# Matmul with rotary embedding on one core: load order, PSUM banks as single tiles, halves and stores at the end

## The chip, the core and the metric

The kernel runs on one core of a Trainium2 chip. The core has five engines that run their own instruction queues side by side and meet at semaphores: TensorE (PE in the profile; matmuls and transposes), VectorE (DVE), ScalarE (ACT), GpSimd (POOL) and SyncE (SP, which here only issues transfers). SBUF is the working memory, PSUM the eight accumulation banks that TensorE writes; a bank holds 512 float32 numbers in each of 128 partitions. Transfers between HBM and SBUF are issued from the queues of SP, ACT and POOL.

The metric is the device time of one execution in microseconds. Six executions of the kernel before took 158.26 to 159.04, with a median of 158.5.

## What is computed

```python
# x: (16, 512, 768)   weight: (768, 768)   cos, sin: (512, 64)   n_heads = 12, all float32
y = np.matmul(x, weight).reshape(batch, seq, n_heads, head_dim)      # head_dim = 64
y1, y2 = y[..., :32], y[..., 32:]
out1 = y1 * cos1 - y2 * sin1      # cos1, sin1: the first 32 columns of cos and sin
out2 = y2 * cos2 + y1 * sin2      # cos2, sin2: the last 32
out = np.concatenate([out1, out2], axis=-1).reshape(batch, seq, hidden)
```

## The kernel before

**Tiles.** The 8192 rows of x are cut into 64 tiles of 128 rows, and the tiles are taken in 32 pairs (n, s), n from 0 to 31 and s 0 or 1. The two tiles of a pair belong to two batches and the same positions, so they share cos and sin. The contraction over 768 is cut into six chunks of 128, named (t, e). Below, x00 is the tile (0, 0), w0 the first chunk of the weight.

**One tile's way.** load() fetches a tile as float32 on SP's queue (L81). cast() makes it float16 (xc), on ACT for all but two early tiles. transpose() turns it with six TensorE transposes into a PSUM tile pt (L124) and copies that to SBUF as xT (L74 on ACT, L76 on VectorE). Every third pair from 8 on (BLOCKS: 8, 11, ... 29) goes another way: POOL's queue loads it as float16 in 32-row blocks (L103), and VectorE transposes it (L131); it costs TensorE nothing. mm() (L167) multiplies one chunk of a tile with one chunk of the weight, w_sb, which cast_w() (L111) has made float16 on VectorE. rope() (L181, VectorE) multiplies the sums in PSUM by cos and by the signed, swapped sin, which gives tq with twice as many columns; add() (L192, POOL) adds the two halves of tq into ov; store() (L241) sends ov to HBM.

**PSUM.** psum() gives a pair one tile of three banks, psy; there are two of these, and pt_pool holds two more banks. The first tile of a pair fills bank 0 and half of bank 1, the second the rest. All three banks come free together, when rope_pair() has read the last of them. The last four pairs (ALONE = 4) take two banks for each tile, 512 columns and 256, from psy or, for three of the eight tiles, from pt_pool (psz in the profile).

**Start.** SP issues the first four x tiles, then w0 in two pieces of 256 and 512 columns, then w1 to w5, cos, sin, and the x tiles of pairs 2 to 6. TensorE begins with matmuls on zeros (warm(), L251, 17 in all), with the transposes of the first four tiles between them. It takes each weight chunk as it arrives: both tiles of pair 0 in every step, tile (1, 0) for four chunks beside them. What is left of pair 1 comes after w5, then pair 2.

**Order.** The order on each engine is the order of the code. In the main loop over pairs 2 to 31 each tile's twelve matmuls are followed by upto("turn", ...) and upto("cast", ...), which emit the transposes and casts of later tiles. Both run ahead by two and four tiles, and from index 31 on by up to six tiles more: the line `k += min(6, max(0, k - 31) // 4)`. The pool of xT tiles has 11 buffers for this. After a pair's matmuls rope_pair() emits the multiplication and the add of the pair; the store of pair n-3 goes out on ACT's queue just before. Pairs 26 and 27 are multiplied and added in halves of 768 columns.

**End.** In the last four pairs each tile is multiplied by rope_alone(), in pieces of 512 and 256 columns, added as 768 columns and stored from ACT. Stores 25 to 27 stand before these on ACT. The last tile (31, 1) is done by rope_last(): the 256 columns by VectorE and POOL with a store on ACT, the 512 by three VectorE instructions (L220 twice, L224) with a store on SP.

Of the kernel before, what the change touches and what calls it, by code (L numbers as in the profile page):

```python
# [10 lines left out]
FP32 = mybir.dt.float32  # L11
FP16 = mybir.dt.float16
# [5 lines left out]
def kernel(  # L18
# [9 lines left out]
    nc = tc.nc  # L28
# [6 lines left out]
    R = 32  # L35
    NQ = P // R
    NT = H // (2 * P)
    SB = S // P
    NP = B * SB // 2
    CHUNKS = [(t, e) for t in range(NT) for e in range(2)]  # L40
# [20 lines left out]
    xpool = ctx.enter_context(tc.tile_pool(name="xpool", bufs=10))  # L61
    bpool = ctx.enter_context(tc.tile_pool(name="bpool", bufs=5))
    cpool = ctx.enter_context(tc.tile_pool(name="cpool", bufs=6))
    tpool = ctx.enter_context(tc.tile_pool(name="tpool", bufs=11))
    rpool = ctx.enter_context(tc.tile_pool(name="rpool", bufs=3))
    opool = ctx.enter_context(tc.tile_pool(name="opool", bufs=6))
    pt_pool = ctx.enter_context(tc.tile_pool(name="pt", bufs=2, space=bass.MemoryType.PSUM))
    py_pool = ctx.enter_context(tc.tile_pool(name="py", bufs=2, space=bass.MemoryType.PSUM))

    xss, xhs, x16, xTT, psys, tqs, ovs = {}, {}, {}, {}, {}, {}, {}  # L70

# [47 lines left out]

    def transpose(n, s, eng):  # L120
        xc = x16.pop((n, s)).rearrange("p (t m e) -> p t e m", t=NT, e=2)
        pt = pt_pool.tile([P, NT, 2, P], FP16, tag="pt", name="pt")
        for t, e in CHUNKS:
            nc.tensor.transpose(pt[:, t, e, :], xc[:, t, e, :], ident)  # L124
        xT = tpool.tile([P, NT, 2, P], FP16, tag="xT", name="xT")
        copy(eng, xT, pt)
        xTT[n, s] = xT
# [12 lines left out]


    def psum(n, s):
        if n < NP - ALONE:
            if n not in psys:
                psys[n] = py_pool.tile([P, 3, 512], FP32, tag="psy", name="psy")
            cut = 512 if s == 0 else 256
            return [
                (psys[n][:, s, ds(s * 256, cut)], 0, cut),
                (psys[n][:, s + 1, 0 : H - cut], cut, H),
            ]  # L150
        if (n, s) not in psys:
            if (2 * (n - NP + ALONE) + s) % 3 == 1:
                psys[n, s] = [
                    pt_pool.tile([P, 512], FP32, tag="pt", name="psz") for _ in (0, 1)
                ]
            else:
                ps = py_pool.tile([P, 3, 512], FP32, tag="psy", name="psy")
                psys[n, s] = [ps[:, 0], ps[:, 1]]
        lo, hi = psys[n, s]
        return [(lo, 0, 512), (hi[:, 0 : H - 512], 512, H)]  # L160

    def mm(n, s, t, e, c0=0, c1=H):
        for k, (ps, lo, hi) in enumerate(psum(n, s)):
# [11 lines left out]
    def rope(n, c0, c1, ps):  # L175
        r = n % SB
        nh = (c1 - c0) // D
        if n not in tqs:
            tqs[n] = rpool.tile([P, 2, 2 * H], FP32, tag="tq", name="tq")
            ovs[n] = opool.tile([P, 2 * H], FP32, tag="ov", name="ov")  # L180
        nc.vector.tensor_tensor(  # L181
            out=tqs[n][:, :, c0:c1].rearrange("p j (h d) -> p j h d", d=D),
            in0=ps.rearrange("p (h d) -> p h d", d=D)
            .unsqueeze(1).broadcast_to((P, 2, nh, D)),
            in1=csn[:, :, r, :].unsqueeze(2).broadcast_to((P, 2, nh, D)),
            op=MULT,
        )

    def add(n, c0, c1, eng):
        w = c1 - c0  # L190
        tq = tqs[n][:, :, ds(c0, w)]
        eng.tensor_tensor(  # L192
            out=ovs[n][:, ds(c0, w)].rearrange("p (h t d) -> p h t d", t=2, d=HD),
            in0=tq[:, 0].rearrange("p (h t d) -> p h t d", t=2, d=HD),
            in1=tq[:, 1].rearrange("p (h t d) -> p h t d", t=2, d=HD)[:, :, ::-1, :],
            op=ADD,
        )

    def rope_pair(n, step=2 * H):
        ps = psys[n].rearrange("p b n -> p (b n)")  # L200
        for c in range(0, 2 * H, step):
            rope(n, c, c + step, ps[:, ds(c, step)])
            add(n, c, c + step, nc.gpsimd)

    def rope_alone(n, s):
        for ps, lo, hi in psum(n, s):
            rope(n, s * H + lo, s * H + hi, ps)

    def rope_last(n, s):
        (ps, _, cut), (pz, _, _) = psum(n, s)
        c0, c1, c2 = s * H, s * H + cut, (s + 1) * H
        rope(n, c1, c2, pz)
        add(n, c1, c2, nc.gpsimd)
        nh = cut // D
        q = tqs[n][:, 1, c0:c1]
        ph = ps.rearrange("p (h d) -> p h d", d=D)
        for o, j in ((q.rearrange("p (h d) -> p h d", d=D), 1), (ph, 0)):
            nc.vector.tensor_tensor(  # L220
                out=o, in0=ph, op=MULT,
                in1=csn[:, j, n % SB, :].unsqueeze(1).broadcast_to((P, nh, D)),
            )
        nc.vector.tensor_tensor(  # L224
            out=ovs[n][:, c0:c1].rearrange("p (h t d) -> p h t d", t=2, d=HD),
            in0=ps.rearrange("p (h t d) -> p h t d", t=2, d=HD),
            in1=q.rearrange("p (h t d) -> p h t d", t=2, d=HD)[:, :, ::-1, :],
            op=ADD,
        )
        store(n, nc.sync, c0, c1)  # L230
        store(n, nc.scalar, c1, c2)

    def store(n, eng, c0=0, c1=2 * H):
        b, r = where(n, 0)
        dst = out.rearrange("b (p r) h -> r p b h", r=SB)[r, :, b : b + 2]
        src = ovs[n].rearrange("p (b h) -> p b h", b=2)
        if c1 - c0 < 2 * H:
            s = c0 // H
            dst = dst[:, s, c0 - s * H : c1 - s * H]
            src = src[:, s, c0 - s * H : c1 - s * H]  # L240
        eng.dma_start(out=dst, in_=src)  # L241
# [5 lines left out]
    def warm(k):  # L247
        for _ in range(k):
            n, b = divmod(opened[0] % 6, 3)
            psum(n, 0)  # L250
            nc.tensor.matmul(  # L251
                psys[n][:, b], cold[:, 0:P], cold, start=True, stop=opened[0] < WARM - 6
            )
            opened[0] += 1

    ctx.enter_context(tc.manual_schedule())

# [8 lines left out]
        pattern=[[-1, P]],  # L266
        channel_multiplier=1,
    )
    for n in (0, 1):
        load_pair(n)  # L270
    load_w(0, 0, 0, 256)
    load_w(0, 0, 256, H)
    for t, e in CHUNKS[1:]:
        load_w(t, e)
    nc.sync.dma_start(out=csn[:, 0], in_=cos.rearrange("(p r) d -> p r d", r=SB))
    nc.sync.dma_start(out=sin_sb, in_=sin.rearrange("(p r) d -> p r d", r=SB))
    for n in range(2, AHEAD):
        load_pair(n)

    done = {"cast": 4, "turn": 4}

    def upto(what, k):
        k += min(6, max(0, k - 31) // 4)
        while done[what] < min(k, 2 * NP):
            n, s = divmod(done[what], 2)
            done[what] += 1
            if what == "cast":
                if n not in BLOCKS:  # L290
                    cast(n, s, nc.scalar)
            elif n in BLOCKS:
                transpose_blocks(n, s)
            else:
                transpose(n, s, nc.scalar)

    warm(10)
    cast(0, 0, nc.vector)
    cast(0, 1, nc.scalar)
    transpose(0, 0, nc.vector)  # L300
    warm(2)
    transpose(0, 1, nc.scalar)
    cast(1, 0, nc.vector)
    cast(1, 1, nc.scalar)
    warm(2)
    transpose(1, 0, nc.vector)
    warm(3)
    for c0, c1 in ((0, 256), (256, H)):
        cast_w(0, 0, c0, c1)
        mm(0, 0, 0, 0, c0, c1)  # L310
        mm(0, 1, 0, 0, c0, c1)
        if c0 == 0:
            transpose(1, 1, nc.scalar)
    for k, c in enumerate(CHUNKS[1:]):
        cast_w(*c)
        if k < 2:
            mm(1, 0, *CHUNKS[k])
        mm(0, 0, *c)
        mm(0, 1, *c)
        if 1 < k < 4:  # L320
            mm(1, 0, *CHUNKS[k])

    nc.vector.tensor_copy(out=csn[:, 1, :, 0:HD], in_=sin_sb[:, :, HD:D])
    nc.vector.tensor_scalar_mul(
# [5 lines left out]
    load_blocks(BLOCKS[0], (1, 3))  # L330
    rope_pair(0)
    upto("cast", 6)
    for c in CHUNKS[4:]:
        mm(1, 0, *c)
    for c in CHUNKS[:3]:
        mm(1, 1, *c)
    upto("turn", 5)
    for c in CHUNKS[3:]:
        mm(1, 1, *c)
    upto("cast", 7)  # L340
    upto("turn", 6)
    upto("cast", 8)
    rope_pair(1)

    for n in range(2, NP):
        load_pair(n + AHEAD - 2)
        for m, quarters in ((n + AHEAD_B, (0, 2)), (n + AHEAD_B - 1, (1, 3))):
            if m > BLOCKS[0]:
                load_blocks(m, quarters)
        for s in (0, 1):  # L350
            for c in CHUNKS:
                mm(n, s, *c)
            upto("turn", 2 * n + s + 3)
            upto("cast", 2 * n + s + 5)
            if n >= NP - ALONE:
                if (n, s) != (NP - 1, 1):
                    rope_alone(n, s)
                    add(n, s * H, (s + 1) * H, nc.gpsimd)
                    store(n, nc.scalar, s * H, (s + 1) * H)
        if n < NP - ALONE:  # L360
            if n >= 3:
                store(n - 3, nc.scalar)
            rope_pair(n, H if n >= NP - ALONE - 2 else 2 * H)
        if n == NP - ALONE - 1:
            for m in (n - 2, n - 1, n):
                store(m, nc.scalar)
    rope_last(NP - 1, 1)


# [1 line left out]
_INS = ['x', 'weight', 'cos', 'sin', 'n_heads']  # L371
# [31 lines left out]
```

## Time and profile before

One execution was profiled. Its time was 158.35 us, and its span, from the first to the last instruction, 156.6.

| what | value |
| --- | --- |
| median of six executions | 158.5 us |
| the profiled execution, time and span | 158.35 us, 156.6 us |
| busy: PE, DVE, ACT, POOL | 95%, 80%, 48%, 82% of the span |
| granted clock of TensorE, mean | 0.989 |
| chain that ended last: PE, DMA, DVE, SP's issues, POOL | 85%, 5%, 4%, 2%, 1% of the span |
| HBM read and written | 27.79 MB, 25.17 MB |

The busy time by stage, from the view that cuts the span into windows (us of busy time):

| window, us | PE | DVE | ACT | POOL | GB/s |
| --- | --- | --- | --- | --- | --- |
| 0 to 9 | 7.59 | 3.31 | 3.75 | 0.70 | 270 |
| 9 to 18.5 | 9.17 | 6.96 | 3.82 | 1.12 | 402 |
| 18.5 to 134 | 115.45 | 96.44 | 66.13 | 108.73 | 324 |
| 134 to 150 | 15.99 | 15.61 | 0.80 | 15.81 | 313 |
| 150 to 156.6 | 0.00 | 2.58 | 0.00 | 2.71 | 199 |

Groups by shape, with the mean duration of one instruction: the multiplication L181 of 3072 products 3.351 us, of 1536 1.752, of 1024 1.216, of 512 0.680 to 0.684; the add L192 of 1536 columns 3.471 us, of 768 1.831, of 256 0.733; ACT's cast of a tile 0.902 and its copy 0.799; VectorE's block transpose 0.689; a cast of a weight chunk 0.560.

How to read it: a busy TensorE in the profile is not TensorE at its peak, since matmuls overlap and their ends are modelled; the distance from one start to the next is what counts. An instruction of VectorE, ACT or POOL starts a little before the one ahead of it ends, as the time lines show. The chain that ended last is followed back from the last instruction, so an engine that is not on it can idle at no cost.

### The profile page before, as it was taken

Reading aid. Unit: us, or ns where it says so; the run is one execution under the profiler, and the core shown is the slowest. Engines: PE = TensorE matmul, PEld = TensorE weight load, DVE = VectorE, ACT = ScalarE, POOL = GpSimd, SP = SyncE. Lnnn points to the kernel's source line nnn. Section 1 sums busy time; section 2 is a strip of 40 time slices with the busy share of each in tenths; the row PEclk is TensorE's granted clock in tenths of the full one; section 3 lists DMA queues with packets and bytes.
Section 4 is the critical chain, followed back from the end, with each engine's and each line's share of the span. In section 5 each row is a group of like instructions: output and inputs, shape, how many; then the busy total and the mean of one; then the engine's idle time right before and its main releaser. Section 6 shows DMA issues by size and latency. Waiting matters only on the chain.

```text
span 156.6 us, 2722 instructions
## 1 busy us (share of the span) xinstructions
PE 148.2 (95%) x1074; PEld 93.4 (60%) x1074; DVE 124.9 (80%) x78; ACT 74.5 (48%) x93; POOL 129.1 (82%) x77
## 2 busy tenths in 40 slices
PE   6999999999999999999999999999999999999930
PEld 2465666666656656666666666766667666655610
DVE  0656967876698699879869798879697899799990
ACT  3340967766525454660755665674746656200000
POOL 1000599999899899899989989997998779999990
PEclk9999999999999999999999999999999999999995
DMA  4999999999999999999999999999995725499655
GB/s 151 349 410 394 402 369 342 340 405 358 364 361 375 316 395 385 296 400 353 287 386 324 318 299 408 291 378 360 300 379 59 298 104 201 166 394 402 248 203 201
DMA packets 25837, 49.99 MB, mean 319 GB/s; under 512 B 10208, under 2 KB 10720, under 8 KB 25824
## 3 DMA queue, kind: packets, MB, share of 16 engines
q10 hardware_dynamic: 8768, 24.91, 41.0%
q1 hardware_dynamic: 8352, 21.76, 37.8%
q0 software_dynamic: 8704, 3.15, 17.3%
q8 instruction: 8, 0.13, 0.3%
q14 instruction: 5, 0.04, 0.1%
HBM read 27.79 MB, written 25.17 MB: 338 GB/s over the span
## 4 chain that ended last, share of the span: by engine, by line
PE 85%; DMA 5%; DVE 4%; SPq 2%; POOL 1%; POOLq 0%; issue 0%; DVEq 0%
PE psy L167 73%; PE pt L124 9%; DMA w_raw<-in_weight_dram 5%; DVE tq L181 3%; PE psz L167 2%; POOL ov L192 1%; SPq L108 1%; SPq L81 1%; POOLq L398 0%; DVE w_sb L111 0%; POOLq L192 0%; DVEq L181 0%
## 5 line engine op out<-in xcount | busy, mean ns | idle before, releaser
L167 PE MATMUL psy<-w_sb,xT 128*128 128x256 f16 (+1 forms) x733 | 126.7, 326 | 0.4 <-DVE w_sb L111 0.2
L181 DVE TENSOR_TENSOR tq<-psy,csn 128x3072 f32<-128x3072 f32 (+3 forms) x40 | 102.8, 2590 | 19.8 <-PE psy L167 19.7
L192 POOL TENSOR_TENSOR ov<-tq 128x1536 f32<-128x1536 f32 (+2 forms) x38 | 110.4, 2924 | 7.0 <-DVE tq L181 6.8
L167 PEld LDWEIGHTS <-xT 128*128 128x128 f16 x769 | 73.3, 98 | 45.7 <-DVE xT L131 0.8
L74 ACT COPY xT<-pt 128x768 f16<-128x768 f16 x46 | 36.4, 799 | 52.2 <-PE pt L124 50.8
L74 ACT CAST xc<-xs 128x768 f16<-128x768 f32 x46 | 40.4, 902 | 7.8 <-DMA xs<-in_x_dram 7.7
L124 PEld LDWEIGHTS <-xc 128*128 128x128 f16 x288 | 20.0, 99 | 6.9 <-DVE xc L76 1.0
L124 PE MATMUL pt<-ident,xc 128*128 128x128 f16 x288 | 23.8, 221 | 0.2 <-DVE xc L76 0.2
L103 POOL DMA_DIRECT2D xh<-in_x_dram x32 | 18.8, 591 | 0.0
L328 POOL COPY mark<-xs 128x1 f32<-128x1 f32 x1 | 0.2, 184 | 16.1 <-DMA xs<-in_x_dram 16.1
L131 DVE STREAM_TRANSPOSE xT<-xh 128x384 f32<-128x384 f32 x16 | 10.6, 689 | 0.0
L251 PE MATMUL psy<-cold 128*128 128x512 f16 x17 | 6.6, 537 | 1.2 <-DVE cold L258 1.2
L167 PE MATMUL psz<-w_sb,xT 128*128 128x512 f16 (+1 forms) x36 | 6.3, 326 | 0.0
L111 DVE CAST w_sb<-w_raw 128x768 f16<-128x768 f32 (+2 forms) x7 | 3.4, 500 | 2.0 <-DMA w_raw<-in_weight_dram 2.0
L181 DVE TENSOR_TENSOR tq<-psz,csn 128x512 f32<-128x512 f32 (+1 forms) x5 | 4.3, 896 | 0.1
L76 DVE CAST xc<-xs 128x768 f16<-128x768 f32 x2 | 1.9, 949 | 2.9 <-DMA xs<-in_x_dram 2.9
L251 PEld LDWEIGHTS <-cold 128*128 128x128 f16 x17 | 2.0, 128 | 3.5 <-issue 2.2
L76 DVE COPY xT<-pt 128x768 f16<-128x768 f16 x2 | 1.1, 558 | 1.9 <-PE pt L124 1.9
L74 ACT ACT_TABLE_LOAD x1 | 1.3, 1283 | 0.7 <-PEq L384 0.7
L258 DVE MEMSET cold<- 128x256 uint32 x1 | 0.3, 272 | 0.9 <-PEq L384 0.9
L224 DVE TENSOR_TENSOR ov<-psz,tq 128x512 f32<-128x512 f32 x1 | 0.7, 690 | 0.0
L220 DVE TENSOR_TENSOR psz<-psz,csn 128x512 f32<-128x512 f32 x1 | 0.7, 687 | 0.0
(9 smaller groups left out, 2.0 us busy)
## 6 DMA issues: line engine op xcount, KB each, us to landing
out_dram<-ov ACTq DMA_DIRECT2D x28, 768.0 KB, 7.6
xs<-in_x_dram SPq DMA_DIRECT2D x48, 384.0 KB, 7.2
xh<-in_x_dram POOLq DMA_DIRECT2D x32, 96.0 KB, 9.3
out_dram<-ov ACTq DMA_DIRECT2D x7, 384.0 KB, 2.4
w_raw<-in_weight_dram SPq DMA_DIRECT2D x5, 384.0 KB, 7.0
w_raw<-in_weight_dram SPq DMA_DIRECT2D x1, 256.0 KB, 5.7
out_dram<-ov SPq DMA_DIRECT2D x1, 256.0 KB, 2.6
w_raw<-in_weight_dram SPq DMA_DIRECT2D x1, 128.0 KB, 5.5
```

The source lines that it names most:

```text
L74: eng.copy(out=o, in_=i_)
L76: eng.tensor_copy(out=o, in_=i_)
L81: nc.sync.dma_start(out=xss[n, s], in_=x[b].rearrange("(p r) h -> r p h", r=SB)[r])
L103: nc.gpsimd.dma_start(out=dst[ts(q, R)], in_=src[r, q])
L108: nc.sync.dma_start(out=w_raw[:, t, e, c0:c1], in_=wv[t, e, :, c0:c1])
L111: nc.vector.tensor_copy(out=w_sb[:, t, e, c0:c1], in_=w_raw[:, t, e, c0:c1])
L124: nc.tensor.transpose(pt[:, t, e, :], xc[:, t, e, :], ident)
L131: nc.vector.transpose(out=xT.bitcast(FP32).rearrange("p t (j a) o -> p t j (a o)", j=NQ), in_=x16.pop((n, s)).bitcast(FP32).rearrange("p ( ...
L167: nc.tensor.matmul(ps[:, a - lo : z - lo], xTT[n, s][:, t, e, :], w_sb[:, t, e, a:z], start=((t, e) == CHUNKS[0] and n > 1), stop=((t, e) ...
L181: nc.vector.tensor_tensor(out=tqs[n][:, :, c0:c1].rearrange("p j (h d) -> p j h d", d=D), in0=ps.rearrange("p (h d) -> p h d", d=D) .unsqu ...
L192: eng.tensor_tensor(out=ovs[n][:, ds(c0, w)].rearrange("p (h t d) -> p h t d", t=2, d=HD), in0=tq[:, 0].rearrange("p (h t d) -> p h t d", ...
L251: nc.tensor.matmul(psys[n][:, b], cold[:, 0:P], cold, start=True, stop=opened[0] < WARM - 6)
```

## The change

It has five parts.

1. Start: SP's order of loads is x00, x01, w0 (undivided), x10, w1, x11, w2, w3, w4, w5, then as before. The matmuls of pair 0 start with w0 after the transposes of pair 0 alone; pair 1's casts (both on VectorE now), transposes and matmuls stand between the weight chunks. The warm matmuls stand 9, 2 and 6, and idle() adds 3 and 2 more matmuls on zeros, between real ones.
2. PSUM: py_pool holds six single banks. rope_bank() multiplies one bank (512 columns, 1024 products) and frees it; the add of a pair stays one instruction (two for pairs 26 and 27). Bank 0 is multiplied after the first tile's matmuls, banks 1 and 2 after the second's.
3. Main loop: the extra run-ahead in upto() is gone, and tpool has 8 buffers in place of 11. In pairs 2 and 3 the matmuls of a tile are emitted by columns, 0 to 256 over all chunks and then the rest, with a transpose between them.
4. The last four pairs: each tile takes two banks of 384 columns, one after the other over all chunks; each half is multiplied and added by itself. Only the last half of the last tile is done by the three VectorE instructions.
5. Late stores, 25 to 27 and those of the single tiles, are issued by SP; ACT issues only that of the last tile's first half.

```diff
-    tpool = ctx.enter_context(tc.tile_pool(name="tpool", bufs=11))
+    tpool = ctx.enter_context(tc.tile_pool(name="tpool", bufs=8))
...
-    py_pool = ctx.enter_context(tc.tile_pool(name="py", bufs=2, space=bass.MemoryType.PSUM))
+    py_pool = ctx.enter_context(tc.tile_pool(name="py", bufs=6, space=bass.MemoryType.PSUM))
...
     def psum(n, s):
...
+        key, banks = (n, 3) if n < NP - ALONE else ((n, s), 2)
+        if key not in psys:
+            psys[key] = [
+                py_pool.tile([P, 512], FP32, tag="psy", name="psy") for _ in range(banks)
             ]
...
+        ps = psys[key]
+        if banks == 2:
+            return [(ps[k][:, 0:HH], k * HH, (k + 1) * HH) for k in (0, 1)]
+        cut = 512 if s == 0 else 256
+        return [(ps[s][:, ds(s * 256, cut)], 0, cut), (ps[s + 1][:, 0 : H - cut], cut, H)]
...
+    def rope_bank(n, b):
+        rope(n, b * 512, (b + 1) * 512, psys[n][b])
+
+    def add_pair(n, step=2 * H):
         for c in range(0, 2 * H, step):
-            rope(n, c, c + step, ps[:, ds(c, step)])
             add(n, c, c + step, nc.gpsimd)
...
+    def idle(k):
+        for _ in range(k):
+            nc.tensor.matmul(psys[1][2], cold[:, 0:P], cold, start=False, stop=False)
...
-    for n in (0, 1):
-        load_pair(n)
-    load_w(0, 0, 0, 256)
-    load_w(0, 0, 256, H)
-    for t, e in CHUNKS[1:]:
-        load_w(t, e)
+
+    load_pair(0)
+    for k, c in enumerate(CHUNKS):
+        load_w(*c)
+        if k < 2:
+            load(1, k)
...
-        k += min(6, max(0, k - 31) // 4)
...
-    warm(10)
+    warm(9)
     cast(0, 0, nc.vector)
     cast(0, 1, nc.scalar)
     transpose(0, 0, nc.vector)
     warm(2)
     transpose(0, 1, nc.scalar)
+    warm(WARM - 11)
+    cast_w(*CHUNKS[0])
+    mm(0, 0, *CHUNKS[0])
+    mm(0, 1, *CHUNKS[0])
     cast(1, 0, nc.vector)
...
+    idle(3)
+    transpose(1, 0, nc.scalar)
+    cast_w(*CHUNKS[1])
+    mm(0, 0, *CHUNKS[1])
+    mm(0, 1, *CHUNKS[1])
+    cast(1, 1, nc.vector)
+    for c in CHUNKS[:2]:
+        mm(1, 0, *c)
+    idle(2)
+    transpose(1, 1, nc.scalar)
+    for k, c in enumerate(CHUNKS[2:]):
         cast_w(*c)
...
         mm(0, 0, *c)
         mm(0, 1, *c)
...
+        if k == 0:
+            mm(1, 0, *c)
+        elif k < 3:
+            mm(1, 1, *CHUNKS[k - 1])
...
         for s in (0, 1):
...
+            i = 2 * n + s
+            if n < 4:
+
+                for c0, c1 in ((0, 256), (256, H)):
+                    for c in CHUNKS:
+                        mm(n, s, *c, c0, c1)
+                    if c0 == 0:
+                        upto("turn", i + 2)
+                        upto("cast", i + 4)
+            elif n < NP - ALONE:
+                for c in CHUNKS:
+                    mm(n, s, *c)
+            upto("turn", i + 3 if i > 6 else 0)
+            upto("cast", i + 5 if i > 6 else 0)
+            if n < NP - ALONE:
+                for b in ((0,), (1, 2))[s]:
+                    rope_bank(n, b)
+                continue
+            for ps, lo, hi in psum(n, s):
+                for c in CHUNKS:
+                    mm(n, s, *c, lo, hi)
+                c0, c1 = s * H + lo, s * H + hi
+                if (n, s, hi) == (NP - 1, 1, H):
+                    rope_last(n, ps, c0, c1)
+                    store(n, nc.sync, c0, c1)
+                    continue
+                rope(n, c0, c1, ps)
+                add(n, c0, c1, nc.gpsimd)
+                if (n, s) == (NP - 1, 1):
+                    store(n, nc.scalar, c0, c1)
+                elif hi == H:
+                    store(n, nc.sync, s * H, (s + 1) * H)
         if n < NP - ALONE:
             if n >= 3:
                 store(n - 3, nc.scalar)
...
+            add_pair(n, H if n >= NP - ALONE - 2 else 2 * H)
         if n == NP - ALONE - 1:
             for m in (n - 2, n - 1, n):
-                store(m, nc.scalar)
-    rope_last(NP - 1, 1)
+                store(m, nc.sync)
```

## The prediction

> **What bounds the kernel now.** I read the chain of waits first, then the engines' time line at both ends, then the groups by shape and the list of DMA issues.
>
> ```profile
> 4.50 7.16 DMA w_raw<-in_weight_dram
> ...
> 12.29 2.82 PE psy L167 x16
> 15.11 0.02 issue
> 15.13 3.37 DVE tq L181
> 18.50 0.04 issue
> 18.55 2.11 PE psy L167 x12
> 20.66 0.34 PE pt L124 x6
> ...
> 41.56 5.93 PE psy L167 x36
> ...
> 101.12 5.85 PE psy L167 x36
> ```
>
> (Start, length, engine, what, how many.) Loads rule to 12.3 us. From 18.55 on the chain is TensorE without a break: 1.95 us for the 12 matmuls of one 128-row tile, 0.336 for the 6 transposes of one. At 41.56 (and again at 54.67 and 67.78) 36 matmuls take 5.92 or 5.93 where at 101.12 they take 5.85: some 0.08 lost three times, at pairs that VectorE transposes. So the middle can give 0.25 at most; all else is at the two ends. Here is the end, by the time line:
>
> ```profile
> 136.00 16.70 POOL L192 TENSOR_TENSOR ov<-tq 128x768 f32<-128x768 f32 x10 [0.19 <-DVE tq L181]
> ...
> 147.88 2.11 PE L167 MATMUL psz<-w_sb,xT 128*128 128x512 f16 x12
> 148.15 1.82 DVE L181 TENSOR_TENSOR tq<-psy,csn 128x1024 f32<-128x1024 f32 x2 [0.19 <-PE psy L167]
> 150.03 0.69 DVE L181 TENSOR_TENSOR tq<-psz,csn 128x512 f32<-128x512 f32 x1
> 150.64 0.68 DVE L220 TENSOR_TENSOR tq<-psz,csn 128x512 f32<-128x512 f32 x1
> 151.24 0.69 DVE L220 TENSOR_TENSOR psz<-psz,csn 128x512 f32<-128x512 f32 x1
> 151.96 0.69 DVE L224 TENSOR_TENSOR ov<-psz,tq 128x512 f32<-128x512 f32 x1
> 152.68 0.35 SPq L241 DMA_DIRECT2D out_dram<-ov  x1
> ```
>
> The last matmul ends at 149.99. Two chains follow: VectorE to 152.65 (store on SP at 152.68) and POOL to 152.70 (store on ACT after it). POOL's ten adds run back to back from 136.00: nine of 768 columns and one of 256, so (16.70-0.73)/9 = 1.774 us from one 768 add to the next. It never catches up; POOL bounds the end as much as TensorE. The list of issues gives the small ACT store 2.7 us to land (about 155.5), and the end of the program 1.1 more: 156.6.
>
> **Change, start of the run.** Loads: the new order is x00, x01, w0, x10, w1, x11, w2 to w5, the same bytes, with one issue less on SP (w0 undivided; SP's issues took 0.33 to 0.70 each and ran ahead of the landings). Casts that wait for weights start at 9.73, 10.71, 11.68, 12.70, 13.67: one load per 0.98. The ten loads end at the same 13.67, cos, sin and the next x tiles behind them as now. So w2 to w5 come no sooner; w0 should come as the third load, between 4.99 (x01) and 9.73 in even steps: about 6.2, x10 7.4, w1 8.5, x11 9.7.
>
> TensorE then goes by its own order. The transposes of x01 end at 7.0 as now. Six fillers of 512 columns follow, 0.216 each ("8.14 0.81 ... x3" is two steps and a duration): to 8.3; the copy of x01's transposes on ACT (0.80, now ended at 8.03) lies under them. Four matmuls of w0 (0.65): 8.95. Three fillers (0.65): 9.6. Transposes of x10 (0.34), cast long before: 9.95. w1 on tile 0 (0.65): 10.6. Now (1,0) needs its transposes copied by ACT: 10.15+0.80+0.15 = 11.1, a wait of 0.5. Two chunks of (1,0): 11.75. Two fillers: 12.2. Transposes of x11: 12.5. From here on it is behind the weights (w2 was cast at 11.3): w2, w3, w4 with three tile-chunks of 0.325 each, 15.45; w5 on tile 0 16.1 (now about 14.93). Four tile-chunks 17.4, transposes of (2,0) 17.75, three tile-chunks 18.7; (2,0) waits for its copy, queued on ACT behind the cast of (2,1) and behind its own transposes: 17.9+0.80+0.15 = 18.85. Now pair 2 starts at 18.55 with the transposes of (2,1) done; they are still due, 0.336. So TensorE is 0.30+0.34 = 0.64 later, although its first real matmul comes 0.8 sooner: 1.08 of fillers and 0.68 of waits for ACT eat it. Bounds: the fillers cost nothing where TensorE would have waited (then 0 later), and everything if a copy comes another 0.5 late (1.1 later). I keep 0.64, since each filler stands between works that are ready.
>
> What the fillers between real work might serve is the clock. In this trace the granted clock stays at 1.00 through the pauses at 8.8 (0.4) and 18.2 (0.35), and matmuls keep their step. The Trainium skill, TensorE: Matmul & The Clock Gate, Part 1, has the gate close after an idle window of some 3.4 us; by that the fillers buy nothing and, as an estimate, the change would be up to 1.08 better without them. No run here shows a longer pause.
>
> **Change, middle.** rope over a pair's 3072 products becomes three of 1024: 3.35 against 3x1.216 less two overlaps of 0.085 = 3.48, so 0.13 more on VectorE per pair, 28 pairs. VectorE is busy 96.4 of the 115.5 us from 18.5 to 134 and would go to 100; bank 0 of a pair is done one tile earlier, so it ends about 1.0 sooner after each pair, and banks come free one by one. Nothing queued behind it waits longer: the transposes of a block tile now stand between two short ropes, a tile and more ahead of their matmuls, which should close the three gaps (-0.25; bounds -0.25 and +0.25 if they come late again). Without the run-ahead in upto(), ACT and PE transposes come two tiles ahead for the whole run; a copy (0.80) and a cast (0.90) per tile of 2.29 leave ACT idle a quarter of the time. 18 instead of 12 matmuls in two tiles are the same columns. Free, with matmul columns as cover. TensorE's last matmul: 149.99+0.64-0.25 = 150.4.
>
> **Change, end.** VectorE: an op of 512 products is 0.68, one of 1024 1.216, so 384 products 0.55. The third half-tile's rope (768, 0.95) starts when its matmuls end, 0.98 before the last, and is done at 150.4; then three ops of 0.55 with starts 0.47 and 0.59 apart: 152.0, store on SP 152.05. That chain gains 0.65 although TensorE is 0.4 later.
>
> POOL: 16 adds become 2 of 768 (pair 27) and 15 of 384. By shape the page has 0.733 for 256 columns, 1.831 for 768, 3.471 for 1536: a straight line, 0.19+2.14 ns a column. A 384 add is 1.007, from start to start 0.95 (less the 0.055 overlap that 1.774 shows). Two of them are 1.90 against 1.774: 0.13 more per tile. What helps is the start: four tiles' transposes, now done before pair 27, move behind it (4x0.336), and pair 27 is roped by bank. Its bank 1 ends 8 tiles (15.6), five transposes (1.7) and 0.15 before the last matmul: 150.4-17.45 = 132.95; rope 1.216: 134.2 instead of 136.0. Then 2x1.774 + 14x0.95 + 1.007: 152.05, against 152.70 now. Bounds for the 384 add from start to start: 0.887 (half a 768, no fixed part) and 1.10 (0.73 for 256 plus a half of it again): end 151.1 to 154.2.
>
> Stores: 25, 26, 27 and the single tiles go from ACT to SP, behind x loads that were all issued long before; each waits for POOL in the same order. ACT's last store has only transposes and copies before it, ended 9 us earlier. Last store 152.08 (ACT, 192 KB); now 128 KB take 2.7, 256 KB 2.6, 384 KB 2.4, so 2.65: 154.75, and 1.1: 155.85.
>
> The Trainium skill (DMA: Bandwidth & Descriptors, Anatomy of one DMA) has 2.0 us fixed plus bytes at 436 GB/s: an estimate of 2.45 for 192 KB. The rows fall with size, since the small ones are last of three in flight; by the page the sum would be 0.2 lower.
>
> **Sum** against the profiled execution (158.35 with a span of 156.57): 155.85 is -0.7, so 157.65. It lies 0.15 under the median 158.5, so I say 157.8.
>
> **Rivals.** (a) *Short adds rule* (slower): if an add of 384 takes 1.05 from start to start, 15 of them put POOL's end at 153.5 and the time at 159.3. It decides from 0.995 on, where the end is as now. For it: POOL is back to back from 136.0 and has nothing to hide behind. Against: three sizes on one line. (b) *The start eats the end*: another copy or cast late by 0.6 before pair 2 moves TensorE and POOL alike: 158.4. For it: ACT casts, copies and waits for loads in one queue. Against: steady tiles leave it slack. (c) *Fillers hidden*: the real loads of x10 and w1 come so late that TensorE waits there anyway, and less is behind after w5: 0.6 better, 157.2; VectorE's 152.0 moves with it. (d) *The order does nothing*: w5 at 13.67 sets pair 2 at 18.55 as before; then the gain is the end's alone, 157.3; it goes with (c).
>
> **How the numbers follow.** Within 0.3% (0.5 us) a run can't be told from no change, so 158.0 and 159.0 are the marks. Forecast 157.8 (own range 157.3 to 158.3): 0.62, of which 0.53 under 158.0. (c) and (d) 0.10. (b) 0.11, some of it over 159. (a) 0.17. Faster 0.63, same 0.17, slower 0.20. Range 157.0 to 159.2.
>
> **What would show it.** First real matmul near 8.3, pair 2 near 18.85; no 5.93 pieces at block pairs; rope of 1024 at 1.22; POOL gapless from about 134.2 with starts 0.95 apart; last matmul about 150.4, POOL's end about 152.05. Wrong if pair 2 starts after 19.4, or if the 384 adds stand over 1.0 apart.

## The result and the profile after

The changed kernel took 157.46 us, the median of 21 executions (156.96 to 157.90). The kernel before took 158.38 in 47 executions beside it (157.98 to 159.07). The ratio is 0.9938, with a 95% interval of 0.9928 to 0.9948: 0.9 us faster, and the measurement can tell that from no change. The forecast was 157.8, in a range of 157.0 to 159.2. The profiled execution took 157.62 with a span of 155.8; the sum had 157.65 and 155.85 for it.

First the start, by the engines' time line (start, busy time, engine, line, operation, what goes into what, how many; in brackets the idle time before and what ended it):

```profile
8.32 0.81 PE L161 MATMUL psy<-w_sb,xT 128*128 128x512 f16 x4
...
8.97 0.81 PE L249 MATMUL psy<-cold 128*128 128x512 f16 x3
...
11.00 0.44 PEld L161 LDWEIGHTS <-xT 128*128 128x128 f16 x4 [0.63 <-ACT xT L75]
...
12.43 5.04 PE L161 MATMUL psy<-w_sb,xT 128*128 128x512 f16 x30
...
15.82 1.88 ACT L75 CAST xc<-xs 128x768 f16<-128x768 f32 x2 [2.39 <-DMA xs<-in_x_dram]
...
17.30 0.50 PE L126 MATMUL pt<-ident,xc 128*128 128x128 f16 x6
...
17.84 0.80 ACT L75 COPY xT<-pt 128x768 f16<-128x768 f16 x1
...
18.69 0.55 PEld L161 LDWEIGHTS <-xT 128*128 128x128 f16 x6 [0.30 <-ACT xT L75]
```

The first matmul with a weight stands at 8.32, the fillers on zeros at 8.97 and (not shown) 11.66, pair 2 at 18.69. The brackets of the two PEld rows are idle time of the weight loads. Counted from one matmul's start to the next, beyond a matmul's own step, TensorE itself waits 0.40 at 11.00 and 0.08 at 18.69, both times for ScalarE's copy of transposed tiles. In between it goes without a pause: 30 matmuls from 12.43, the transposes of (2, 0) from 17.30 to 17.80, the last chunks of (1, 1). On ScalarE, x20 lands at 15.80 and x21 at 16.78; each is cast as it lands, the second to 17.70, and the copy for (2, 0) starts at 17.84, 0.04 after its transposes end. So in this execution TensorE's own work came last at pair 2, and ScalarE's casts were done 0.1 before it.

The middle and the end, by the chain of waits (start, length, engine, what, how many):

```profile
12.59 4.87 PE psy L161 x30
17.47 0.34 PE pt L126 x6
17.80 1.72 PE psy L161 x12
...
42.08 5.85 PE psy L161 x36
...
131.08 1.75 PE psy L161 x11
...
132.85 1.06 DVE tq L175
...
134.21 1.06 POOL ov L186
...
148.35 2.92 POOL ov L186 x3
```

The first three rows are the start again: the chain passes pair 2 on TensorE, not on ScalarE. The pieces of 36 matmuls at block pairs all take 5.85 now. The chain leaves TensorE at 132.8, for VectorE's multiplication of pair 27's second bank, and ends with GpSimd's adds. Before, it stayed with TensorE to 148.06, two microseconds before the last matmul's end:

```profile
148.15 1.83 DVE tq L181 x2
...
150.01 2.01 POOL ov L192 x2
```

The changed end by the time line:

```profile
150.34 0.56 DVE L212 TENSOR_TENSOR tq<-psy,csn 128x384 f32<-128x384 f32 x1
150.81 0.56 DVE L212 TENSOR_TENSOR psy<-psy,csn 128x384 f32<-128x384 f32 x1
151.40 0.56 DVE L216 TENSOR_TENSOR ov<-psy,tq 128x384 f32<-128x384 f32 x1
152.25 0.35 ACTq L231 DMA_DIRECT2D out_dram<-ov  x1
```

VectorE's three last instructions begin at 150.34, just after the last matmul's end (150.305), and end at 151.96. GpSimd's last add ends at 152.215, and ScalarE issues the last store at 152.25. It lands at 154.69.

**Where the time came from.** For the profiled execution of each kernel, the time splits at the end of the last matmul into what the start and middle decide and a tail. (The two kernels with late stores on ScalarE are left out: TensorE pauses there after pair 28, their last matmuls end at 153.88 and 152.05, and GpSimd catches up in the pause, so that their tails are 6.58 and 6.57.) "First cast of pair 2" is the start of ScalarE's cast of x20, which follows x20's landing at once.

| kernel | time of the profile | first cast of pair 2 | pair 2 starts | last matmul ends | tail (time less last matmul) |
| --- | --- | --- | --- | --- | --- |
| before | 158.35 | 15.39 | 18.55 | 149.995 | 8.36 |
| changed | 157.62 | 15.82 | 18.70 | 150.305 | 7.32 |
| changed, run again | 157.31 | 15.69 | 18.39 | 149.998 | 7.31 |
| without fillers | 157.48 | 15.96 | 18.58 | 150.185 | 7.30 |
| without fillers, copy first | 156.62 | 15.19 | 17.54 | 149.291 | 7.33 |
| start of before | 157.00 | 15.61 | 18.41 | 149.671 | 7.33 |
| start of before, run again | 157.26 | 15.84 | 18.65 | 149.915 | 7.35 |
| start of before, fewer halved adds | 156.82 | 15.60 | 18.39 | 149.649 | 7.17 |
| whole adds in pairs 28 to 30 | 157.54 | 16.02 | 18.65 | 150.261 | 7.28 |
| run-ahead back | 158.43 | 15.35 | 18.02 | 149.627 | 8.80 |
| bank 0 multiplied late | 158.77 | 15.93 | 18.65 | 150.263 | 8.51 |
| old halves | 157.97 | 15.59 | 18.22 | 149.832 | 8.14 |

So the change is a tail shorter by 1.04 and a last matmul 0.31 later. In all kernels with the changed end untouched the tail is 7.30 to 7.35; what differs between executions of one kernel is when the first loads land. In the two of the changed kernel the first matmul with a weight starts at 8.32 and 8.01, x20's cast at 15.82 and 15.69, and everything behind moves by 0.3. That makes the tail the sharp instrument here, and the start a blunt one.

### The profile page after: what moved, and what is told of

Its sections match the earlier page's. It is cut to its first block, busy times and chain, and to the rows that moved or that the text cites. A ratio compares the mean times of both kernels' runs of the same rounds, so it can differ in the third digit from the quotient of the medians.

```text
span 155.8 us, 2832 instructions
## 1 busy us (share of the span) xinstructions
PE 148.8 (96%) x1090; PEld 95.0 (61%) x1090; DVE 129.5 (83%) x131; ACT 75.1 (48%) x93; POOL 130.3 (84%) x84
## 4 chain that ended last, share of the span: by engine, by line
PE 84%; POOL 9%; issue 2%; DVE 1%; POOLq 1%; ACT 1%
PE psy L161 70%; PE pt L126 10%; POOL ov L186 9%; PE psy L241 4%; PE psy L249 1%; DVE tq L175 1%; POOLq L412 1%; ACT xT L75 1%; DVE cold L253 0%
## 5 line engine op out<-in xcount | busy, mean ns | idle before, releaser
L161 PE MATMUL psy<-w_sb,xT 128*128 128x256 f16 (+2 forms) x780 | 132.8, 323 | 0.2 <-ACT xT L75 0.2
L175 DVE TENSOR_TENSOR tq<-psy,csn 128x1024 f32<-128x1024 f32 (+1 forms) x99 | 111.8, 1170 | 14.6 <-PE psy L161 13.5
L161 PEld LDWEIGHTS <-xT 128*128 128x128 f16 x780 | 74.2, 98 | 43.7 <-ACT xT L75 0.9
L75 ACT COPY xT<-pt 128x768 f16<-128x768 f16 x47 | 37.5, 799 | 63.9 <-PE pt L126 63.7
L75 ACT CAST xc<-xs 128x768 f16<-128x768 f32 x45 | 39.7, 903 | 5.6 <-DMA xs<-in_x_dram 5.5
L241 PE MATMUL psy<-cold 128*128 128x512 f16 x17 | 6.5, 538 | 1.2 <-DVE cold L253 1.2
L77 DVE CAST xc<-xs 128x768 f16<-128x768 f32 x3 | 2.9, 953 | 4.6 <-DMA xs<-in_x_dram 4.6
L112 DVE CAST w_sb<-w_raw 128x768 f16<-128x768 f32 x6 | 3.3, 558 | 1.3 <-DMA w_raw<-in_weight_dram 1.3
L249 PE MATMUL psy<-cold 128*128 128x512 f16 x5 | 1.4, 379 | 0.0
L216 DVE TENSOR_TENSOR ov<-psy,tq 128x384 f32<-128x384 f32 x1 | 0.6, 557 | 0.0
```

The source lines that it names most:

```text
L75: eng.copy(out=o, in_=i_)
L77: eng.tensor_copy(out=o, in_=i_)
L112: nc.vector.tensor_copy(out=w_sb[:, t, e, c0:c1], in_=w_raw[:, t, e, c0:c1])
L161: nc.tensor.matmul(ps[:, a - lo : z - lo], xTT[n, s][:, t, e, :], w_sb[:, t, e, a:z], start=((t, e) == CHUNKS[0] and n > 1), stop=((t, e) ...
L175: nc.vector.tensor_tensor(out=tqs[n][:, :, c0:c1].rearrange("p j (h d) -> p j h d", d=D), in0=ps.rearrange("p (h d) -> p h d", d=D) .unsqu ...
L241: nc.tensor.matmul(psys[n][b], cold[:, 0:P], cold, start=True, stop=opened[0] < WARM - 6)
```

## The experiments

Before's medians beside the three groups of runs were 158.62, 158.42 and 158.40. Ratios are against these.

### The changed kernel once more

No edit, as a control beside the runs that follow.

> The changed kernel itself once more, as the measure on this chip for the three beside it: ratio 0.994, span 155.8.

Measured: 157.37, ratio 0.9929 [0.9910, 0.9947].

### Run-ahead back

```diff
-    tpool = ctx.enter_context(tc.tile_pool(name="tpool", bufs=8))
+    tpool = ctx.enter_context(tc.tile_pool(name="tpool", bufs=11))
...
+        k += min(6, max(0, k - 31) // 4)
```

> The changed kernel with the run-ahead of transposes and casts from index 31 on put back, and 11 xT buffers. Theory A (four tiles' transposes behind pair 27 let POOL's last chain start sooner): TensorE's last matmul stays at 150.3 to 150.4, bank 1 of pair 27 is done 1.3 later, POOL's chain starts at about 135.5 instead of 134.21 and ends at 153.5, span 157.1, time 158.7, ratio 1.002. Rival (the run-ahead only moves work that is hidden): POOL's end 152.2, time 157.4, ratio 0.994.

Measured: 158.95, ratio 1.0028 [1.0015, 1.0041]. GpSimd's rows of the time line:

```profile
134.87 17.94 POOL L186 TENSOR_TENSOR ov<-tq 128x768 f32<-128x768 f32 x17 [0.65 <-POOL ov L186]
```

The 17 adds take 17.94 without a gap (18.01 in the changed kernel), but begin 14.76 before the end of the last matmul (149.627), not 16.10 as in the changed kernel: 1.34, which is four tiles' transposes of 0.336. They stand ahead of pair 27 again, and GpSimd pays for it at the end.

### Bank 0 late

```diff
-                for b in ((0,), (1, 2))[s]:
+                for b in ((), (1, 0, 2))[s]:
```

> The changed kernel with each main-loop pair's banks multiplied in the order 1, 0, 2, so that bank 0 waits for the second tile as it did when the pair was one instruction. Theory A (bank by bank lets VectorE and so POOL finish a pair 1.1 sooner): no new waits of TensorE, last matmul 150.3, POOL's chain starts at about 135.3 and ends at 153.3, span 156.9, time 158.5, ratio 1.001. Rival (the multiplication by bank frees banks for TensorE and that is its worth): last matmul over 150.8.

Measured: 158.61, ratio 1.0012 [1.0000, 1.0024].

```profile
135.37 17.99 POOL L186 TENSOR_TENSOR ov<-tq 128x768 f32<-128x768 f32 x17 [0.31 <-POOL ov L186]
```

The chain begins 1.2 later against the last matmul, one multiplication of 1024 products, and ends as much later. From the start of pair 2 to the end of the last matmul it is 131.61, as in the changed kernel: in the main loop, when the banks come free costs TensorE nothing.

### Old halves

```diff
-            return [(ps[k][:, 0:HH], k * HH, (k + 1) * HH) for k in (0, 1)]
+            return [(ps[0], 0, 512), (ps[1][:, 0 : H - 512], 512, H)]
...
-            for ps, lo, hi in psum(n, s):
-                for c in CHUNKS:
-                    mm(n, s, *c, lo, hi)
+            for c in CHUNKS:
+                mm(n, s, *c)
...
+            add(n, c0, c2, nc.gpsimd)
```

> The changed kernel with the last four pairs cut as before: 512 and 256 columns, both matmuls of a chunk one after the other, one add of 768 columns for a tile, and three VectorE instructions of 512 on the last tile; stores stay on SP but for the last 256 columns. Theory A: VectorE ends 2.65 after the last matmul (150.3) instead of 1.66, at 152.95, POOL at about 152.7, last store 153.0, span 156.6, time 158.3, ratio 1.000. Rival (the early start of POOL's chain is the whole gain and the halves nothing): span 155.8 to 156.0, ratio 0.994 to 0.996.

Measured: 158.22, ratio 0.9984 [0.9971, 0.9997].

```profile
145.55 1.82 POOL L186 TENSOR_TENSOR ov<-tq 128x768 f32<-128x768 f32 x1 [0.53 <-DVE tq L175]
```

```profile
149.87 0.69 DVE L175 TENSOR_TENSOR tq<-psy,csn 128x512 f32<-128x512 f32 x1 [0.17 <-PE psy L161]
...
151.80 0.69 DVE L216 TENSOR_TENSOR ov<-psy,tq 128x512 f32<-128x512 f32 x1
```

Both engines are late now: VectorE ends at 152.49, 2.66 after the last matmul as in the kernel before, and GpSimd at 152.33. GpSimd starts early and then waits for VectorE (0.53 before the add shown, 0.34 and 0.40 before two others), whose products of a tile come only when the tile is whole.

### Whole adds in pairs 28 to 30

```diff
-                add(n, c0, c1, nc.gpsimd)
+                if n == NP - 1:
+                    add(n, c0, c1, nc.gpsimd)
+                elif hi == H:
+                    add(n, s * H, (s + 1) * H, nc.gpsimd)
```

> The changed kernel with the adds of pairs 28 to 30 taken as 768 columns for a tile (after its second half is multiplied) instead of two of 384; pair 31 keeps its halves. Theory A (VectorE feeds the last adds about as fast as POOL takes them, so the fixed part of six more adds, 6x0.13, is not on the path): POOL waits for VectorE between adds, its end stays within 0.2 of 152.2, time 157.3 to 157.6, ratio 0.993 to 0.995. Rival (short adds bound the end): POOL's end 0.8 sooner, and the time limited by VectorE's end at 151.96, some 156.9 to 157.2.

Measured: 157.28, ratio 0.9912 [0.9893, 0.9931].

```profile
139.90 7.16 POOL L186 TENSOR_TENSOR ov<-tq 128x768 f32<-128x768 f32 x4 [0.35 <-DVE tq L175]
147.44 4.68 POOL L186 TENSOR_TENSOR ov<-tq 128x768 f32<-128x768 f32 x4 [0.37 <-DVE tq L175]
```

Each pair of short adds costs two steps of 0.960 against 1.774 for a whole one; six of them fewer should have saved GpSimd some 0.8 if it were alone. It gives them back in waits for VectorE and ends 1.86 after the last matmul in place of 1.91. So six whole adds win next to nothing; that four, in pairs 28 and 29 alone, win a little is shown by the last experiment.

### Late stores on ScalarE, and two of its parts

All of the late stores back on ScalarE's queue:

```diff
-                    store(n, nc.sync, s * H, (s + 1) * H)
+                    store(n, nc.scalar, s * H, (s + 1) * H)
...
-                store(m, nc.sync)
+                store(m, nc.scalar)
```

> The changed kernel with the late stores (25 to 27 and those of the single tiles) issued by ACT, as before. Theory A (the stores wait for POOL's adds and now stand ahead of ACT's copies for tiles 60 to 63, which the missing run-ahead left late): TensorE waits for those copies, 1 to 2 us in all from 141 us on, last matmul 151.3 to 152.3, time 158.5 to 159.4, ratio 1.000 to 1.006. Rival (only the issuing time moves): last matmul 150.3, time 157.4 to 157.6, ratio 0.994.

Then only the second of these two edits, the stores of pairs 25 to 27:

> Only the stores of pairs 25 to 27 on ScalarE's queue again, those of the single tiles on SP. Theory A (store 27, which waits for GpSimd, keeps the cast of tile 60 behind it, and that alone stops TensorE for over 2 us, after which it goes at half step): as with all late stores on ScalarE, a pause of 2.2 near 136.7, then matmuls of 384 columns 0.32 apart for some 3 us, last matmul near 153.5, time 158.3 to 158.8. Rival (the single tiles' stores do part of it): under 158.0. Rival (the half step was an accident of that one run): the pause, but matmuls 0.16 apart after it, last matmul near 152, time 157.5 to 158.

Measured: 158.68, ratio 1.0028 [0.9997, 1.0060], and 158.67, ratio 1.0043 [1.0005, 1.0081]. The time line of the second:

```profile
134.17 3.68 ACTq L231 DMA_DIRECT2D out_dram<-ov  x2
137.89 1.71 ACT L75 CAST xc<-xs 128x768 f16<-128x768 f32 x2 [4.00 <-POOL ov L186]
```

```profile
138.84 0.51 PE L126 MATMUL pt<-ident,xc 128*128 128x128 f16 x6 [1.94 <-ACT xc L75]
```

Store 27 waits for GpSimd's add until 137.5, the cast of tile 60 stands behind it on ScalarE and runs at 137.89, its transposes at 138.84: TensorE starts nothing for 2.26 us, and its last matmul ends at 152.05. The move to SP is a needed part of the change, since the cast now comes behind this store where the run-ahead used to bring it ahead. I had expected copies to be late; it was a cast. The single tiles' stores add nothing.

What follows the pause is not the same each time. In windows of time (five engines' busy time, then the granted clock, the share of DMA and GB/s), the first kernel and then the second:

```profile
139.00:143.00 4.00, 4.00 (x19) 2.10 (x20) 1.59 (x2) 2.00 (x3) 3.04 (x4) 0.57 1.02 397
```

```profile
139.00:143.00 4.00, 4.00 (x34) 2.64 (x33) 2.70 (x4) 3.42 (x5) 3.81 (x5) 1.00 1.02 396
```

After the same pause (2.255 and 2.262 us) TensorE did 19 instructions in 4 us at a granted clock of 0.57 in one execution and 34 at 1.00 in the other; in the first, matmuls of 384 columns stand 0.32 apart in place of 0.162 until 142.94, and the last ends at 153.88. Over all executions, 3 of 12 and 5 of 12 show a mean clock of 0.982 to 0.984 and take 160.3 to 160.8; the rest show 0.992 to 0.998 and take 158.2 to 159.0. So my expectation of the second run was right on the pause and its cause, and wrong that half step always follows. The last rival was right that it is a matter of the single execution, but put the time too low: the pause alone makes it 158.2 to 159.0. The rival of the single tiles' stores is out.

### Without the fillers

```diff
-    idle(3)
...
-    idle(2)
```

> The changed kernel without the five matmuls on zeros that stand between real ones (idle). Theory A (TensorE is behind the weights there, so a filler is paid in full until a wait for ACT swallows it): pair 2 starts at about 18.0 instead of 18.70, the last matmul and POOL's end move by the same 0.7 (150.3 to 149.6, 152.2 to 151.5), span about 155.1, time 156.8, ratio to before 0.990. Rival (the fillers hold the clock): matmul steps of 0.43 for 512 columns come back somewhere between 9 and 19 us, pair 2 starts after 18.7, time 157.5 or more.

Measured: 157.38, ratio 0.9919 [0.9901, 0.9937]: a miss. The clock stays full, but pair 2 starts at 18.58, and the chain of waits reaches it by loads and ScalarE now:

```profile
10.29 6.61 DMA xs<-in_x_dram
...
16.92 0.90 ACT xc L75
17.82 0.71 ACT xT L75
```

x21 lands at 16.90, and behind its cast comes the copy for (2, 0). From the first matmul with a weight to pair 2 TensorE waits 1.26 in all, counted from start to start, against 0.48 with the fillers: 0.35 of it for this copy, 0.25 for the cast of x10 and 0.20 for that of w1, the rest in smaller pieces. So 0.78 of the fillers' 1.08 came back as waits. The first matmul stood 0.17 later in this execution, and pair 2 comes 0.12 sooner.

### Without the fillers, the copy first

```diff
-    upto("cast", 6)
+    upto("cast", 5)
...
+    upto("cast", 6)
```

(and the two idle() lines out as above; the cast of (2, 1) now stands behind the copy of (2, 0).)

> The changed kernel without the fillers, and with the cast of tile (2,1) emitted behind the copy of tile (2,0)'s transposes on ScalarE. Theory A (pair 2's start is bound by the landing of x20 and by ScalarE's order, cast of (2,1) ahead of the copy of (2,0)): the wait of 0.56 shrinks to 0.1 or less, pair 2 starts near 18.2 if x20 lands near 15.9; perhaps 0.15 comes back as a wait for the copy of (2,1); time 156.9 to 157.2. Rival (the transposes of (2,0) themselves come late because of x20's landing, so the order on ScalarE does nothing): pair 2 at 18.6, 157.4.

Measured: 157.15, ratio 0.9922 [0.9899, 0.9945].

```profile
16.69 0.80 ACT L75 COPY xT<-pt 128x768 f16<-128x768 f16 x1 [0.60 <-PE pt L126]
...
17.38 0.90 ACT L75 CAST xc<-xs 128x768 f16<-128x768 f32 x1
17.54 0.55 PEld L161 LDWEIGHTS <-xT 128*128 128x128 f16 x6 [0.30 <-ACT xT L75]
```

From x20's cast to pair 2 it is 2.35 now, against 2.62 without this move, so the order on ScalarE was worth 0.27: the copy no longer stands behind a cast that waits for x21. The rest of the early 17.54 is x20's landing, 0.77 earlier in this execution. A wait of 0.13 for the cast of (2, 1) comes back. In the ratio this can't be told from the run above.

### The start of before

The loads, casts and matmuls before pair 2 as in the kernel before, and the casts and transposes ahead of the main loop as there; everything else as changed. The core of a longer diff:

```diff
-    load_pair(0)
-    for k, c in enumerate(CHUNKS):
-        load_w(*c)
-        if k < 2:
-            load(1, k)
+    for n in (0, 1):
+        load_pair(n)
+    load_w(0, 0, 0, 256)
+    load_w(0, 0, 256, H)
+    for t, e in CHUNKS[1:]:
+        load_w(t, e)
...
+    upto("cast", 7)
+    upto("turn", 6)
+    upto("cast", 8)
```

> The changed kernel with the start of the kernel before: order of loads, w0 in two pieces, order of casts, transposes and matmuls up to pair 2; all else as changed. Theory A (the new start costs about 0.6, the middle and the end gain): pair 2 starts at about 18.35 with both its tiles transposed, no pieces of 5.93 in the middle, last matmul about 149.5, POOL's end about 151.3, span 154.9, time 156.5, ratio 0.988. Rival (feeding TensorE sooner is what gained): pair 2 at 18.55 as before, last matmul later than 150.3, time 157.5 to 158.4.

> The kernel with the start of before and the rest of the change, once more, as the neighbour of the next run on the same chip. Theory A (the new start costs about 0.6): 157.0, the last matmul near 149.7, GpSimd's chain gapless from about 133.6 to 151.6, VectorE's end 0.25 sooner. Rival (the earlier 157.0 was a lucky landing of pair 2's loads): 157.4, as the changed kernel.

Measured: 157.00, ratio 0.9897 [0.9879, 0.9914], and, on another chip, 157.21, ratio 0.9930 [0.9908, 0.9951].

```profile
18.41 2.78 PE L161 MATMUL psy<-w_sb,xT 128*128 128x256 f16 x24
```

Here 24 matmuls follow before the next transposes, where the changed kernel has 6 and then those of (2, 1): pair 2 starts at the same time, but with 0.336 less to do. The medians (157.46 and 157.37 against 157.00 and 157.21) put the new start at 0.3 us too dear. The first of the two runs alone had suggested 0.6 by its ratio; the second does not bear that out, and the intervals of the second and of the changed kernel overlap. Counted from x20's cast to the end of the last matmul, which takes out that load's landing, the three kernels with the start of before need 134.05 to 134.08, and those with the changed start and its fillers 134.25 to 134.33 (134.49 in the changed kernel's first profile): 0.2 to 0.3 dearer, or 0.4.

The kernel before needs 134.61 by the same count, although its start is the same. There pair 2 waited 0.34 for VectorE to finish the one multiplication of pair 0 that held all three banks (the prediction's rows at 15.13 and 18.55); with single banks the row above shows no wait. This gain of the banks at the start was not in the working, and the middle adds 0.19.

### The start of before, fewer halved adds

As the last, and in the loop over the last four pairs:

```diff
-                add(n, c0, c1, nc.gpsimd)
+                if n >= NP - 2:
+                    add(n, c0, c1, nc.gpsimd)
+                elif hi == H:
+                    add(n, s * H, (s + 1) * H, nc.gpsimd)
```

> The start of before, and the adds of pairs 28 and 29 whole (768 columns), in halves only for pairs 30 and 31. Theory A (GpSimd's chain of adds, gapless, ends the run once the last matmul is early; each pair of short adds costs 0.13 more than a whole one): the chain starts near 133.6 and ends about 0.4 sooner than with halves throughout, near 151.2 to 151.3, level with VectorE's end; time 0.25 to 0.35 under the run beside it. Rival (a whole add waits for VectorE as in the run with whole adds of 28 to 30, so nothing is won): the same time within 0.1.

Measured: 156.89, ratio 0.9904 [0.9879, 0.9928], the lowest median of all, 0.32 under the run beside it. By the tail, which doesn't depend on landings, the edit is worth 0.17 and not 0.4.

```profile
139.28 11.14 POOL L186 TENSOR_TENSOR ov<-tq 128x768 f32<-128x768 f32 x9 [0.33 <-DVE tq L175]
```

Four whole adds save GpSimd four times 0.14, but more than half of that goes into a wait of 0.33 for VectorE at 139.28; GpSimd's end (151.378) is then level with VectorE's (151.31), as expected. Between the expectation and its rival, the truth lay in the middle.

## Why the prediction was right, point by point

**The sum and its two halves.** The tail was forecast at 157.65 - 150.4 = 7.25 and measured 7.32; the last matmul at 150.4, measured 150.305. The direction and the place, a gain at the end and a smaller loss at the start, held. That the sum meets the profiled time within 0.03 is partly luck: pair 2 came 0.15 sooner than forecast and the last store took 0.2 less, while the middle gained 0.07 less and GpSimd's end lay 0.26 further behind the last matmul (1.91 and not 1.65). Against the median of 157.46 the forecast of 157.8 is 0.34 high.

**The end, VectorE.** Forecast 152.0, measured 151.96. With the old halves the same chain is 2.66 after the last matmul in place of 1.66.

**The end, GpSimd.** The chain was to begin at 134.2 and begins at 134.21, gapless, with the short adds 0.960 from start to start (0.95 forecast, on the straight line through three sizes). It ends at 152.215, 0.16 late: 14 steps of 0.960 are 0.14 more. (The adds before are the ten that the working counts first, not 16; the sum for the new chain has the right 17.) Both things named as its help hold by themselves: the four tiles' transposes behind pair 27 are worth 1.3 at its end, the early bank 0 another 1.2. Undoing any one of three parts (run-ahead, bank order, halves) costs 0.8 to 1.5 of a tail that gained 1.04 in all, so their worths don't add: the end has two chains, and each part is needed for one of them not to be the later.

**The last store.** 2.65 was taken from before's rows; the store took 154.69 - 152.25 = 2.44, so the rows were 0.2 too high, and this made up for GpSimd's 0.16. The Trainium skill, DMA: Bandwidth & Descriptors, section Anatomy of one DMA, has the figures behind the estimate of 2.45, but gives them for transfers that GpSimd issues; this store went out on ScalarE's queue. That the two numbers meet here does not show that the page's sum holds for such stores: the list of issues has 2.2 for SP's last store of the same 192 KB.

**The middle.** From pair 2 to the last matmul it was 131.45 with both tiles of pair 2 transposed, and is 131.61 with only the first: 0.18 gained for the same work, against 0.25 forecast. With the start of before, and so with both tiles transposed, it is 131.26. No piece of 5.93 is left.

**The start: the term that was off.** The working had TensorE behind by 0.64, 0.30 of it at pair 2, with "1.08 of fillers and 0.68 of waits for ACT" eating an early first matmul. In the profiled execution TensorE's part of this came as worked out: the first matmul with a weight at 8.32 (8.3), every step from there to the end of (2, 0)'s transposes at 17.80 (17.75) within 0.1, although the loads came later than the working had them (w5's cast at 14.11 and not 13.67, x20's at 15.82 and not 15.39). What was too dear is the way from there to pair 2: besides the copy's own 0.80, 0.30 was allowed between the transposes and the first matmul, and it took 0.09, so pair 2 stood at 18.70 and not 18.85.

What the working did not see is how close a second line runs: x21's landing, its cast and then the copy on ScalarE. In the profiles of this load order with the fillers, pair 2 starts 0.08 to 0.23 after TensorE would have been ready, and 2.63 to 2.88 after x20's cast. So taking the fillers out, which the working put at up to 1.08, brought pair 2 only 0.12 sooner, and the first half of rival (c) was right: without them TensorE waits, 0.45 for the casts of x10 and w1 and 0.35 for the copy. The second half, 0.6 better, did not come, because the second line holds pair 2. The whole start costs 0.2 to 0.3 by medians and by the count from x20's cast, no more than the 0.336 of the transposes of (2, 1) still due.

**What was costed at nothing.** The late stores on SP cost nothing, as forecast. What the working left out is what they would have cost where they were: without the run-ahead a cast stands behind store 27 on ScalarE, and without the move the whole gain is gone.

**The clock.** The Trainium skill, TensorE: Matmul & The Clock Gate, Part 1, has the gate close after an idle window of about 3.4 us, and says that the window runs freely. By that the fillers buy nothing for the clock, and without them the granted clock is as full (0.994 in the mean). But a pause of 2.26 us, below that length, was followed by half step in one of the two profiled executions, and by their mean clock and time in 8 of 24.

The traces' record of clock changes shows where the two profiles differ. In all fourteen traces a stretch at full clock is a whole number of steps of 3.413 us long (mostly 43 or 44). Counted in such steps, TensorE's pause in the run that went to half step lies in one step, 136.14 to 139.55, with 1.93 us idle by the profile, and the half clock is granted from 139.55 to 142.96. In the other run the pause is parted at 138.01, into 1.11 and 0.83 us, and the clock stays. At the ends of the runs one step with 1.81 us idle left the clock up (whole adds), one with 2.39 took it down (start of before). So here a step need not be idle throughout, and where the pause falls in it decided; two profiled pauses are few for a rule.

**The rivals.** (a) decides from 0.995 a step, and the step is 0.960; what is more, six whole adds gain 0.05 at GpSimd's end and four 0.17 of the tail, since VectorE is nearly as late. (b) did not happen. (c) is answered above. (d) would have kept pair 2 at 18.55 at no cost; pair 2 does start near there, but with the transposes of (2, 1) still to do.

Not measured is the changed start with the copy first beside fewer halved adds; whether it goes below 156.9 is open.

## What to carry to other kernels

Split the profiled time at the last matmul: the tail here repeats within 0.05 us from chip to chip, while the start moves by up to half a microsecond with the landing of the first loads, so parts of a change are judged by the tail and not by the medians alone. Before work on TensorE's order is priced, follow every line that the first steady tile waits for, and not only the one that comes last: where a second one is 0.1 behind, taking 1.08 us of work out of the first gained 0.12. A store that waits for another engine should not stand in the queue of an engine that still has casts to do.

## What the runs showed of the hardware

After a pause of 2.26 us TensorE went at half step for 3.41 us in one of two profiled executions, and by mean clock and time in 8 of 24, worth some 2 us of the time. The profiled cases differ in where the pause lies in steps of 3.413 us: 1.93 us idle in one step took the clock down, 1.11 and 0.83 in two did not.

Landings of the first loads differ between executions of one kernel: x20's cast began between 15.19 and 16.02 in the ten profiles with the new load order (those of the table and the two with late stores on ScalarE), and x21 landed 0.96 to 1.01 behind x20.
